# A gated linear unit on one core: the stores of the odd tiles 1 to 29 issued from the sync queue, ahead of the load that waits for the same products

## The chip, the cores and the metric

The kernel runs on one core of a Trainium2 chip. The metric is the device time of one execution in microseconds (us). One execution was profiled as well; the profile's times count from the start of its span.

## The reference

The input x is an array of 8192 x 8192 float32 (268.44 MB). Its left half a is gated by its right half b; the output is 8192 x 4096 float32 (134.22 MB):

```
a, b = np.split(x, 2, axis=-1)
return a * (1 / (1 + np.exp(-b)))
```

Every element is read once and written once, and little is done with it in between.

## The kernel before, in words

**Tiles.** The rows are cut into 32 tiles of 256 rows, two rows to each of the 128 partitions. A tile's load brings 64 KB to each partition (8.39 MB), its store takes 32 KB from each (4.19 MB). In HBM the two rows of a partition lie side by side, so a partition's part of a tile is one contiguous piece. There are two buffers for loads (xs) and two for results (os), used in turn (SLOTS = 2, line 19): tile i uses buffer i % 2.

**What is done with a tile** (function `work`, lines 72 to 100). ScalarE applies the sigmoid to the right half in place (line 92). Then the product is written to the result buffer (line 97) in two pieces: GpSimd takes 1536 of each partition's 8192 results, VectorE the other 6656, one after the other (line 98 makes VectorE's piece follow GpSimd's). On tile 1 VectorE does both pieces. Tiles 0 and 31 are done in four quarters, each with its own activation and product on VectorE, so that work begins and ends on less than a whole tile.

**The waits.** The activation of a middle tile i waits for two things: that load i has landed, and that store i-2 has left the result buffer. They are joined by an empty instruction on TensorE (line 87), which the profile shows as PEldq or PEq. The load of tile i+2 (line 63) goes into the buffer of tile i, so it waits until the products of tile i are done. The store of tile i (line 68) waits for the same products. `place` (line 48) keeps only the waits that are named and keeps each engine's instructions in program order.

**Queues.** Loads are issued from SyncE (nc.sync; the profile's SPq), stores from ScalarE (nc.scalar; ACTq). The profile numbers the DMA queues by who issued: q1 holds SyncE's transfers and q10 ScalarE's. Both are worked off by the same 16 DMA engines.

**Order.** The loop at line 104 goes over the tiles. For each tile it lays down the work, then the load of tile i+2 (line 112), then the stores that are still due (lines 113 and 114). Tile 0's result is stored in two halves, tile 31's in one half and two quarters (lines 37 and 39); all other tiles have one load and one store.

**Start and end.** `_launch_early` (line 117) moves the first load ahead of the kernel's opening barrier. `_close_on_sync` (line 130) rewrites the closing: GpSimd waits for all semaphores but that of the last store from ScalarE's queue, and SyncE waits for that one.

Of the kernel before, what the change touches and what calls it, by code (L numbers as in the profile page):

```python
# [8 lines left out]
def _tiles(ctx, tc, x, out):  # L9
    nc = tc.nc  # L10
    P = nc.NUM_PARTITIONS
    DEP = mybir.DependencyInfo(mybir.DependencyClass.Sync, mybir.DependencyReason.DATA)
    fp32 = mybir.dt.float32
    SIG = mybir.ActivationFunctionType.Sigmoid

    n_rows, n_cols = x.shape
    half = n_cols // 2
    R = 2
    SLOTS = 2
    n_tiles = n_rows // (P * R)  # L20
    x_g = x.rearrange("(g p h r) m -> g h p (r m)", p=P, h=2, r=R)
    out_g = out.rearrange("(g p h r) m -> g h p (r m)", p=P, h=2, r=R)

    pool = ctx.enter_context(tc.tile_pool(name="io", bufs=1))
    xs = [pool.tile([P, R * n_cols], fp32, name=f"x_sb{k}") for k in range(SLOTS)]
    os = [pool.tile([P, R * half], fp32, name=f"o_sb{k}") for k in range(SLOTS)]

    whole = [(0, 8)]
    rows = [(0, 4), (4, 8)]
    cut = half // 16 * 3  # L30
    few_and_most = [(0, 8, 0, cut), (0, 8, cut, half)]
    fourths = [(k, k + 2, k % 4 * half // 4, (k % 4 + 2) * half // 4) for k in range(0, 8, 2)]
    loads = [whole] * n_tiles
    works = [few_and_most] * n_tiles
    stores = [whole] * n_tiles
    behind = [0] * n_tiles
    loads[0] = stores[0] = rows
    works[0] = works[-1] = fourths
    stores[-1] = [(0, 4), (4, 6), (6, 8)]
    behind[-1] = 1  # L40

    def meet(a, b):
        return a[0] < b[1] and b[0] < a[1]

    traced = [[] for _ in range(SLOTS)]
    load_of, mul_of, store_of = {}, {}, {}

    def place(i, ins, *needs):


        kept = {n.ins.name for n in needs}
        for e in traced[i % SLOTS]:
            if e.ins.name not in kept:
                tc.declare_no_dep(ins.ins, e.ins, reason="follows from the waits that are kept")
        traced[i % SLOTS].append(ins)
        tc.keep_in_program_order(ins)
        return ins

    def load(i):
        for lo, hi in loads[i]:  # L60
            c = slice(lo * n_cols // 4, hi * n_cols // 4)
            free = [m for w, m in mul_of.get(i - SLOTS, []) if meet(w, (lo, hi))]
            ins = nc.sync.dma_start(out=xs[i % SLOTS][:, c], in_=x_g[i // 2, i % 2, :, c])  # L63
            load_of.setdefault(i, []).append(((lo, hi), place(i, ins, *free)))

    def store(i, lo, hi):
        c = slice(lo * half // 4, hi * half // 4)
        ins = nc.scalar.dma_start(out=out_g[i // 2, i % 2, :, c], in_=os[i % SLOTS][:, c])  # L68
        done = [m for w, m in mul_of[i] if meet(w, (lo, hi))]
        store_of.setdefault(i, []).append(((lo, hi), place(i, ins, *done)))  # L70

    def work(i, lo, hi, near, far):

        rows = xs[i % SLOTS].rearrange("p (r h m) -> p r h m", r=R, h=2)
        packed = os[i % SLOTS].rearrange("p (r m) -> p r m", r=R)
        r, c = slice(lo // 4, (hi + 3) // 4), slice(near, far)
        b = rows[:, r, 1, c]
        landed = [s for w, s in load_of[i] if meet(w, (lo, hi))]
        gone = [s for w, s in store_of.get(i - SLOTS, []) if meet(w, (lo, hi))]
        middle = 0 < i < n_tiles - 1  # L80
        rest = middle and near
        if rest:
            before = mul_of[i].pop()[1]
        else:
            g = rows[:, r, 1, :] if middle else b
            if middle and gone:
                met = nc.tensor.nop(nofuse=True)  # L87
                for n in (*landed, *gone):
                    tc.add_manual_dep(met.ins, n.ins.name, DEP, reason="joins the waits")
                place(i, met, *landed, *gone)  # L90
                landed = [met]
            before = nc.scalar.activation(out=g, in_=g, func=SIG)  # L92
            for n in landed:
                tc.add_manual_dep(before.ins, n.ins.name, DEP, reason="both have landed")
            place(i, before, *landed)
        engine = nc.gpsimd if far == cut and i > 1 else nc.vector
        mul = engine.tensor_mul(out=packed[:, r, c], in0=rows[:, r, 0, c], in1=b)  # L97
        tc.add_manual_dep(mul.ins, before.ins.name, DEP, reason="follows the gate, or the first columns")
        place(i, mul, before, *(() if middle else gone))
        mul_of.setdefault(i, []).append(((lo, hi), mul))  # L100

    for i in range(SLOTS):
        load(i)
    for i in range(n_tiles):
        due = list(stores[i])
        for k, piece in enumerate(works[i]):
            work(i, *piece)
            ready = works[i][k - behind[i]][1] if k >= behind[i] else 0
            while len(stores[i]) > 1 and k < len(works[i]) - 1 and due[0][1] <= ready:
                store(i, *due.pop(0))  # L110
        if i + SLOTS < n_tiles:
            load(i + SLOTS)
        for lo, hi in due:
            store(i, lo, hi)


def _launch_early(nc):
# [68 lines left out]
@with_exitstack  # L186
def kernel(
    ctx: ExitStack,
    tc: tile.TileContext,
    x: bass.AP,  # L190
    out: bass.AP,
):
    nc = tc.nc
    with ExitStack() as pools:
        _tiles(pools, tc, x, out)
    tc.close()
    tc.compile()
    _launch_early(nc)
    _close_on_sync(nc)
# [30 lines left out]
```

## Time and profile before

| what | value | where |
|---|---|---|
| time, median of 3 runs | 932.57 us (932.52 to 932.69) | the runs |
| the profiled execution's own time | 932.44 us | the runs |
| its span | 931.1 us | the page's head |
| VectorE busy | 232.5 us, 25% | page, part 1 |
| ScalarE busy | 227.0 us, 24% | page, part 1 |
| GpSimd busy | 99.3 us, 11% | page, part 1 |
| bytes moved | 402.67 MB, 432 GB/s over the span | page, parts 2 and 3 |
| activation of a middle tile | 7.03 us | groups by form, line 92 |
| product on GpSimd, on VectorE | 3.42 us, 7.09 us | groups by form, line 97 |
| a load, from issue to landing | 40.0 us, median | page, part 6 |
| a store of a whole tile, from issue to landing | 40.2 us, median | page, part 6 |

The page's first part gives the busy time of the engines that compute: none is busy for more than a quarter of the span. Its second and third parts are about the DMA engines, which all loads and stores share: packets, bytes, and the time for which packets were under way. The chain of waits (part 4) starts at the last instruction and goes back, at each step to what released it. A DMA can be asked about in narrow windows too: how many packets of which queue started in it. A transfer's time "to landing" counts from its issue, so it holds the time in which its packets stood behind others.

### The profile page before, as it was taken

The page shows a single profiled execution, that of the slowest core. Times are in us where ns is not written, and L with a number is a line of the kernel's source. Part 1 is how long each engine was busy: PE and PEld are TensorE (multiplying, and loading weights), DVE is VectorE, ACT ScalarE, POOL GpSimd, SP SyncE. Part 2 cuts the span into 40 slices and gives each one's busy share as a digit, 9 for nine tenths or more (in the row PEclk, how much of TensorE's full clock was granted, in tenths as well). Part 3 has the DMA queues.
Part 4 walks back from the last instruction along what each step waited for, and adds up shares of the span by engine and source line. Part 5 has one row for each costly group of instructions (what it writes and reads, how often), then busy time and mean ns, then how long its engine had stood idle before and what let it go on. Part 6 is the DMA issues. An engine that isn't in the chain of part 4 may idle for free.

```text
span 931.1 us, 299 instructions
## 1 busy us (share of the span) xinstructions
DVE 232.5 (25%) x39; ACT 227.0 (24%) x39; POOL 99.3 (11%) x33
## 2 busy tenths in 40 slices
DVE  1133203332023320233302333023330233311333
ACT  2123332033320333202332023320233202333023
POOL 0001110111101111011110111101111011110110
DMA  9999999999999999999999999999999999999998
GB/s 405 450 442 414 428 450 425 453 405 428 450 428 450 410 469 405 428 450 428 450 405 459 420 428 451 425 450 408 431 448 428 450 408 467 408 428 450 427 452 383
DMA packets 9793, 402.67 MB, mean 432 GB/s; under 512 B 1088, under 2 KB 1088, under 8 KB 1088
## 3 DMA queue, kind: packets, MB, share of 16 engines
q1 hardware_dynamic: 4752, 268.44, 66.6%
q10 hardware_dynamic: 5040, 134.22, 33.4%
q14 instruction: 1, 0.01, 0.0%
HBM read 268.44 MB, written 134.22 MB: 432 GB/s over the span
## 4 chain that ended last, share of the span: by engine, by line
DMA 69%; DVE 12%; ACT 12%; POOL 5%; issue 0%; PEldq 0%; ACTq 0%; SPq 0%
DMA out_dram<-o_sb 60%; DVE o_sb L97 12%; ACT x_sb L92 12%; DMA x_sb<-in_x_dram 9%; POOL o_sb L97 5%; PEldq L87 0%; ACTq L68 0%; SPq L63 0%
## 5 line engine op out<-in xcount | busy, mean ns | idle before, releaser
L97 DVE TENSOR_TENSOR o_sb<-x_sb 128x6656 f32<-128x6656 f32 (+2 forms) x39 | 232.5, 5969 | 690.3 <-POOL o_sb L97 632.7
L92 ACT ACTIVATE x_sb<-x_sb 128x8192 f32<-128x8192 f32 (+1 forms) x38 | 225.7, 5949 | 692.7 <-PEq L87 632.9
L97 POOL TENSOR_TENSOR o_sb<-x_sb 128x1536 f32<-128x1536 f32 x29 | 99.1, 3417 | 793.9 <-ACT x_sb L92 793.9
L92 ACT ACT_TABLE_LOAD x1 | 1.3, 1283 | 0.8 <-PEq L214 0.8
L214 POOL MEMSET const-float32-0.0<- 128x1 f32 x1 | 0.1, 99 | 0.2 <-issue 0.2
L214 POOL MEMSET const-bfloat16-1.0<- 128x1 bf16 x1 | 0.1, 103 | 0.0
L214 POOL MEMSET const-uint8-127<- 128x1 uint8 x1 | 0.1, 103 | 0.0
L214 POOL MEMSET const-float32-1.0<- 128x1 f32 x1 | 0.1, 99 | 0.0
## 6 DMA issues: line engine op xcount, KB each, us to landing
out_dram<-o_sb ACTq DMA_DIRECT2D x30, 4096.0 KB, 40.2
x_sb<-in_x_dram SPq DMA_DIRECT2D x2, 4096.0 KB, 16.6
out_dram<-o_sb ACTq DMA_DIRECT2D x3, 2048.0 KB, 27.8
out_dram<-o_sb ACTq DMA_DIRECT2D x2, 1024.0 KB, 8.3
x_sb<-in_x_dram SPq DMA_DIRECT2D x31, 40.0
```

The costliest lines, as they stand in the source:

```text
L92: before = nc.scalar.activation(out=g, in_=g, func=SIG)
L97: mul = engine.tensor_mul(out=packed[:, r, c], in0=rows[:, r, 0, c], in1=b)
L214: nc = _bacc.Bacc("TRN2", target_bir_lowering=False, num_devices=1)
```

## The change

The stores of tiles 1, 3, 5 to 29 are issued from SyncE instead of ScalarE. For odd tiles the stores that are due are laid down before the load of tile i+2; for even tiles they stay behind it, as before. Tile 31 is odd, but its stores stay on ScalarE's queue; it has no load behind it. The waits that each store and load carry are the same as before.

```
     def store(i, lo, hi):
         c = slice(lo * half // 4, hi * half // 4)
-        ins = nc.scalar.dma_start(out=out_g[i // 2, i % 2, :, c], in_=os[i % SLOTS][:, c])
+        odd = i % 2 and i < n_tiles - 1
+        ins = (nc.sync if odd else nc.scalar).dma_start(out=out_g[i // 2, i % 2, :, c], in_=os[i % SLOTS][:, c])
...
+        if i % 2:
+            for lo, hi in due:
+                store(i, lo, hi)
         if i + SLOTS < n_tiles:
             load(i + SLOTS)
-        for lo, hi in due:
-            store(i, lo, hi)
+        if i % 2 == 0:
+            for lo, hi in due:
+                store(i, lo, hi)
```

## The prediction

> **What bounds the kernel now.** I read the page's DMA queues first, then the stages, then the chain of waits, then the DMA queues in narrow windows. A queue name is that of an issuer: q1 carries what SyncE issues, q10 what ScalarE issues. The columns are packets, MB, and the time the packets took as a share of 16 engines' span.
>
> ```profile
> q1 hardware_dynamic: 4752, 268.44, 66.6%
> q10 hardware_dynamic: 5040, 134.22, 33.4%
> ```
>
> The two shares fill all 16 engines. Each DMA has 16 small completion packets (the page counts 1088 under 512 B for 68 DMAs). q1 keeps 4752 - 33x16 = 4224 data packets of 64 KB (the first two loads: half), q10 5040 - 35x16 = 4480 of 32 KB for whole stores. So each engine gets 8 packets of a load and 8 of a store. 66.6% of 16 x 931.1 us over 4096 packets' worth of 64 KB is 2.42 us each; 33.4% over 4096 worth of 32 KB is 1.215 us. A byte costs the same in either direction and on either queue.
>
> ```profile
> 842.61:871.60 28.99, 7.09 (x1) 7.03 (x1) 3.42 (x1) 1.00 1.00 434
> 871.60:900.61 29.01, 7.09 (x1) 7.03 (x1) 3.42 (x1) 1.00 1.00 434
> ```
>
> In these two stages (one tile each, from the end of one tile's products to the next) the last columns are granted clock, DMA share and GB/s: the DMA engines are at 1.00 and 434 GB/s. 12.58 MB a tile at 434 is 29.0 us, which is the tile's period. So the middle is bound by bytes. What waits there wait only for their turn:
>
> ```profile
> 853.81 0.03 issue
> 853.84 0.06 PEldq L87
> 853.90 0.02 issue
> 853.92 7.04 ACT x_sb L92
> 860.96 0.07 issue
> 861.03 3.43 POOL o_sb L97
> 864.46 0.02 issue
> 864.48 7.10 DVE o_sb L97
> 871.58 0.02 issue
> 871.60 40.04 DMA x_sb<-in_x_dram
> 911.64 0.02 issue
> ```
>
> This is the end of the chain (start, us, what). From a landing to the end of that tile's products is 17.79 us (853.81 to 871.60). The load then issued, tile 31's, needs 40.04 us; at the next tile's products, 900.61, 11.03 us of it are left. Only a DMA engine with nothing to move can lengthen this kernel.
>
> **Who is served first.** Load and store of a tile are issued together and land after 40.0 and 40.2 us: one packet of each in turn. In the window 882.8 to 900.61 both queues start 80 packets. Two rows show how a queue that had been empty joins. The first load is issued at 0.00; no packet starts before 0.97, all 16 engines have started one by 1.6. Tile 0's first store is issued at 18.57, while q1 is busy:
>
> ```profile
> q1 hardware_dynamic: 62, 2.03, 98.1%
> ```
>
> That is the whole of 18.57 to 23.5: loads alone. In 23.5 to 24.0 only q10 starts packets, 16. Available after 0.98 to 1.6 us, as the first load, it was at 19.6 to 20.2; then the packet in service and one more load packet, 64 KB, went first. I read from this that the next packet is already taken when one starts.
>
> **The change, part by part.** 15 stores (tiles 1, 3, ... 29) leave ScalarE's queue, 0.36 us of issue each, and stand on SyncE's queue before the load that needs the same products. What it costs the engines: nothing; SyncE has only issues to do and waits 858.2 us for products, ScalarE is idle 690 us. The load behind the store is issued some 0.36 us later, against 11.03 us of backlog. The store's wait for the products is one that the load behind it has anyway, so nobody is newly held; semaphore instructions beside the issues take 17 ns. On ScalarE the next activation no longer stands behind an odd tile's store; it waits for its own load, which lands later than those products (853.90 against the products' end at 842.61), so that gains nothing.
>
> What moves is the order in the DMA queues. Call an even tile's product end T. Its store starts on an empty q10, soon after T. q1 holds the rest of the odd tile's load, then the load issued at T. An odd tile adds store, then load, both on q1. From about T+33 (8 rounds of 3.63 us after joining) q10 is empty, and q1 alone works through the load, the odd store (8 x 1.215 = 9.7 us) and the next load. Bytes are the same, so two tiles still take 58.0 us as long as q1 doesn't run dry. The even tile's load lands at T+40.2 (its 29.0 us with the store, 11.03 of backlog, a completion), its products end at T+58.0. The odd tile's load lands at about T+14.7 (below), its products end at T+32.5, and at that point 40.2 - 32.5 = 7.7 us are left in the queues against 11.03 now. Less the 0.98 to 1.6 us to a first packet, that still covers. **Middle: 0.** The product ends stand 32.5 and 25.5 us apart instead of 29.0.
>
> One thing in the middle no row shows: a store behind a load in the same queue, with the other queue empty. Below: the engines are at share 1.00 and each byte costs the same both ways, so there is nothing to win. Above: a stop as long as a first packet, 0.98 to 1.6 us, at each of 30 boundaries. Nearest rows: two loads in one queue (4.19 MB each) let their activations start at 12.10 and 21.82, 9.72 us apart, where the bytes at 434 GB/s take 9.67. The last stores follow each other as closely, and in the middle each engine changes direction at every packet. I take 0, and keep 0.1 us each (3 us) for the range.
>
> The Trainium skill, DMA: Bandwidth & Descriptors, section Anatomy of one DMA (SWDGE path), gives each DMA of that path, GpSimd's, some 2 us of fixed cost, mostly a write receipt. If that stopped a queue that is alone, 30 boundaries would give an estimated 60 us. The 9.72 us row speaks against it, for loads.
>
> **The end** is where order counts. Today load 31 lands at 911.64 and store 30, queued behind store 29, has only begun: all its 128 data packets start within 910.6 to 920.3. That work lies beside tile 31's first products:
>
> ```profile
> 911.66 5.51 ACT L92 ACTIVATE x_sb<-x_sb 128x2048 f32<-128x2048 f32 x3 [21.70 <-DMA x_sb<-in_x_dram]
> 913.61 6.70 DVE L97 TENSOR_TENSOR o_sb<-x_sb 128x2048 f32<-128x2048 f32 x3 [13.02 <-ACT x_sb L92]
> 918.13 0.34 ACTq L68 DMA_DIRECT2D out_dram<-o_sb  x1
> ```
>
> Tile 31's first store is issued 6.49 us after the landing, and could start on the last engine at 6.49 + 1.6 = 8.1; store 30 lasts until 9.3 (9.7 us less the 0.35 us from last packets, 911.3, to landing). So the engines never stop, with 1.2 us to spare.
>
> Changed, store 29 is finished by T30 (it went before load 31 on q1) and store 30 meets load 31 alone, packet by packet. Step by step:
> 1. q1 has been alone for 17.79 + 0.35 = 18.1 us at T30 on the last engine: 9.7 for store 29, 8.4 for load 31, that is 3.5 of its 8 packets. 11.03 us remain, as now.
> 2. Store 30 is available 1.6 us later on that engine, in the fifth packet (on the first engine, 0.6 us ahead in its packets, after 0.98 us: also the fifth). The sixth is already taken. So a store packet comes before the seventh, before the eighth, and before load 31's completion packet, which takes a turn (as now: of q1's completions none starts before 910.6, though its last data packets start by 908.5). Three store packets: 3 x 1.215 = 3.6 us.
> 3. Load 31 lands at T30 + 14.7. Of store 30 five packets are left, 6.1 us, so the engines run dry 5.7 us after the landing.
> 4. Tile 31's first store starts at 8.1 after it. The engines stand still for **2.4 us**. Nothing else is left to move. Behind that the last 4.19 MB take their 9.7 us as before; the later pieces, products ready at 8.7 and 11.1 after the landing, are in time.
>
> With n store packets ahead of the completion the stop is 1.215n - 1.3: n=2 gives 1.1, n=3 2.4, n=4 3.6. n=4 needs the store available 0.4 us earlier than I take, n=2 some 2 us later. I choose 3, by the row of tile 0's store. If T30 itself stays where the bytes put it, the sum is 0 + 2.4.
>
> **Sum.** The profiled execution took 932.44 us, 931.1 of it span, 1.34 around it. 932.44 + 2.4 = 934.8; the median of the runs is 0.13 above the profiled execution, so **935.0**.
>
> **Rivals.**
> - *No change that can be measured* (the bound used for the chances is 0.2%, 1.87 us, about what a measurement of this kernel can tell from no change). Mechanism: store 30 is admitted late enough at T30 that load 31 keeps its place, n of 2 or less; the stop is then 1.1 us or nothing, the time 932.6 to 933.7. It decides at 1.215n - 1.3 = 1.87. For: the first store of tile 0 needed 5 us. Against: that wait is explained by two packets, and here two are allowed for. Chance 0.15. The Trainium skill, DMA: Bandwidth & Descriptors, section Issuing engines are not separate DMA queues, speaks for this: it says that choosing another issuer only saves the sequencer's time. By it the time would stay at 932.6. The rows agree for the middle; at the end they show two queues that take turns, and there it leaves out the order.
> - *Stops at the 30 boundaries* on a queue that is alone: 0.98 to 1.6 us each give 29 to 48 us more, 964 to 983. Nothing covers them, since the engines are the bound. For: no row has a store and a load behind each other in one queue. Against: the load rows and the last stores. 0.08, and something small of this kind (0.1 us each, 938.0) lies inside the forecast's upper end.
> - *Faster*: runs of one direction move bytes faster than alternating packets. 0.3% more rate would give 929.8. Against: 2.42 us for 64 KB and 1.215 for 32 KB are the same rate, and loads alone at the start run no faster. 0.05.
> - *The forecast*, n of 3 or 4 and up to 0.1 us a boundary: 0.72.
>
> Slower by over 0.2%: 0.72 + 0.08 = 0.80; within: 0.15; faster: 0.05. The range from 933.1 (n=2, with the shorter first packet of 0.98 us: 932.57 + 0.5) to 938.0 (932.57 + 2.4 + 3) leaves out some 0.1 below and 0.08 above.
>
> **What would show it.** Middle: product ends alternating near 32.5 and 25.5 us, 58.0 a pair, DMA share 1.00 and 434 GB/s in a pair; odd stores landing 17 us after issue, even ones 33. A pair above 58.1 means boundary stops. End: load 31 landing near 14.7 us after T30, a gap of 2 to 4 us without packets before tile 31's first store packet, q10's packets starting some 4 us or more after T30. Wrong would be: T30 later than 901 (the middle lost), an end as dense as now (admission late), or more than 434 GB/s in a pair.

## The result and the profile after

The changed kernel took 940.81 us (median of 4 runs, 940.22 to 946.33), the kernel before 932.63: ratio 1.0101, 95% interval 1.0085 to 1.0117. I had forecast 935.0, with 933.1 to 938.0 as range. The sign was right, the size wrong by more than a factor of three: 8.2 us lost instead of 2.4.

The profiled execution happened to be the longest of the four (946.33); the other three took 940.22 to 940.90. So I read the page from it, and the stages from a second profile of the same kernel (run e4_again below), whose execution took 940.43 us with a span of 939.1. First the DMA queues of the page, as before: packets, MB, share of 16 engines' span.

```profile
q1 hardware_dynamic: 6912, 331.35, 81.9%
q10 hardware_dynamic: 2880, 71.30, 17.5%
```

The bytes have moved over as they should: 63 MB from q10 to q1. But the shares now sum to 99.4% of 945.0 us, 939 us of packets per engine, where before they were 100.0% of 931.1. So the same packets took some 8 us longer, and some 6 us of the span no packet ran. (A share is given to 0.1%, which is 0.9 us.) Two losses, then: **longer packets** and **time without packets**. In the second profile's page the shares are 81.9 and 17.6% of 939.1: 934.4 us of packets (3.3 more than before) and 4.7 us without.

Stages of that second profile: two tiles early, two tiles late, and the end (start:end, length, busy times, clock, DMA share, GB/s).

```profile
121.44:181.73 60.29, 14.18 (x2) 14.06 (x2) 6.83 (x2) 1.00 0.99 428
706.29:764.43 58.14, 14.18 (x2) 14.06 (x2) 6.83 (x2) 1.00 1.00 433
880.96:939.10 58.14, 16.08 (x5) 14.45 (x5) 3.42 (x1) 1.00 0.89 385
```

The share stays near 1.00 in the middle, yet a pair of tiles takes 60.3 us early and 58.1 late, against 58.0 before. A share of 1.00 says that a packet is always under way; it doesn't say how long the packet takes. Nor is the length of a pair the mean loss of the engines: of the load that the early pair waits for, 15 engines write their completion in the window 160 to 162, and the tile's activation starts only at 164.06, when the last engine is done. At the end the share is 0.89. The order of the middle is as forecast: odd stores land 16.2 us after issue (forecast 17), even ones 32.7 (33) in the page's DMA issues.

The end, in the chain of waits of the second profile (start, us, what):

```profile
881.35 39.88 DMA x_sb<-in_x_dram
921.23 0.02 issue
921.25 1.92 ACT x_sb L93
```

Tile 30's products end at 905.07, so load 31 lands 16.2 us later; the forecast had 14.7, before had 11.03. Then the DMA queues in the window 925.75 to 928.5, at its head line:

```profile
DMA packets 0, 0.00 MB, mean 0 GB/s; under 512 B 0, under 2 KB 0, under 8 KB 0
```

For 2.75 us no packet starts on any engine, and the last one before it, which started by 924.55 and takes 1.2 us, is over: tile 31's first store, issued at 927.72, only begins after it. That is the stop of the forecast. But most engines had stopped well before 925.75, because they no longer finish together. Load 31's 16 completion packets, one from each engine, in the kernel before (window 910.6 to 911.4, q1):

```profile
q1 hardware_dynamic: 16, 0.00, 1.1%
```

and in the second profile of the change, in the windows 915 to 918.95 and 915 to 920.95 (all queues; the small ones are the completions, and none of another DMA falls into these windows):

```profile
DMA packets 63, 1.77 MB, mean 448 GB/s; under 512 B 14, under 2 KB 14, under 8 KB 14
DMA packets 88, 2.52 MB, mean 424 GB/s; under 512 B 16, under 2 KB 16, under 8 KB 16
```

Before, all 16 engines end a load within 0.8 us. After, 14 are done by 918.95 and the last two only two us later; the whole spread is near 6 us. The landing is that of the last engine.

### The profile page after: what moved, and what is told of

It is laid out like the page before. It is cut to its first block, busy times and chain, and to the rows that moved or that the text cites. A ratio compares the mean times of both kernels' runs of the same rounds, so it can differ in the third digit from the quotient of the medians.

```text
span 945.0 us, 285 instructions
## 1 busy us (share of the span) xinstructions
DVE 232.5 (25%) x39; ACT 227.0 (24%) x39; POOL 99.3 (11%) x33
## 3 DMA queue, kind: packets, MB, share of 16 engines
q1 hardware_dynamic: 6912, 331.35, 81.9%
## 4 chain that ended last, share of the span: by engine, by line
DMA 69%; DVE 12%; ACT 12%; POOL 5%; SPq 1%; issue 0%; PEldq 0%; ACTq 0%
DMA x_sb<-in_x_dram 69%; DVE o_sb L98 12%; ACT x_sb L93 12%; POOL o_sb L98 5%; SPq L69 1%; PEldq L88 0%; ACTq L69 0%; SPq L63 0%
## 6 DMA issues: line engine op xcount, KB each, us to landing
out_dram<-o_sb SPq DMA_DIRECT2D x15, 4096.0 KB, 16.2
out_dram<-o_sb ACTq DMA_DIRECT2D x15, 4096.0 KB, 32.7
```

## The experiments

All are written on the changed kernel with a function `moved(i)` in place of the test for odd tiles, if not said otherwise: a moved tile's store goes over the sync queue ahead of the load, another's over the scalar queue behind it. Three more kernels leave stores out and move fewer bytes; their times stand in the text.

| run | what goes over the sync queue | us | against before, same chip | ratio, 95% |
|---|---|---|---|---|
| e4_again | the change again | 940.86 | +8.3 | 1.0075 to 1.0126 |
| e1_only29 | store 29 alone | 937.93 | +5.3 | 1.0042 to 1.0072 |
| e2_not29 | odd stores 1 to 27 | 938.12 (to 943.35) | +5.5 | 1.0045 to 1.0098 |
| e3_all_sync | stores 1 to 30 | 938.20 | +5.6 | 1.0044 to 1.0074 |
| f1_only15 | store 15 alone | 934.54 | +1.9 | 1.0013 to 1.0031 |
| f2_last_two | stores 29 and 30 | 935.29 | +2.7 | 1.0017 to 1.0038 |
| f3_behind | odd stores, behind the load | 974.11 | +41.5 | 1.0437 to 1.0472 |
| h1_and_30 | the change and store 30 | 937.92 | +5.3 | 1.0045 to 1.0073 |
| h2_half | odd stores 1 to 13 | 936.98 | +4.4 | 1.0036 to 1.0061 |

### End and middle apart

```
 def moved(i): return i == 29                     # e1_only29
 def moved(i): return i % 2 == 1 and i < 29       # e2_not29
```

> Only the store of tile 29 goes over the sync queue, ahead of load 31; all else as before. This is the end of the change by itself. Theory A (joining: whenever the scalar queue has run empty and gets a store again while loads run on the sync queue, a load packet on every engine takes some 0.5 us longer; and the engines drift apart by it): one such joining, engines still in step, so the stop at the end as I predicted, 2.4 us, plus 0.5: about 935.5. Theory B (the end alone costs what was measured, joining nothing): 938 to 941. Theory C (a load behind a store in one queue stops the engines): 935 plus one boundary or two, under 937.

> The stores of the odd tiles 1 to 27 go over the sync queue, that of tile 29 stays on the scalar queue: the middle of the change by itself, the end as before. Theory A (joining, 14 times 0.5 us): about 7 us slower than before, 938 to 940, and no stop before tile 31's stores. Theory B (the end alone): 932.6. Theory C (28 boundaries in one queue): 5 to 8 us, like A; the next run tells C from A.

One moved store at the end costs 5.3 us; A gave 2.9, C less than 4.4, B 5.4 or more, so none of the three ranges holds it. The middle alone costs 5.5 us (four executions, 937.71 to 943.35), so B (the end is all) falls. The end by itself, in the chain of e1_only29:

```profile
872.25 46.48 DMA x_sb<-in_x_dram
918.73 0.02 issue
```

Load 31 needs 46.48 us where it needed 40.04. From tile 30's products at 900.88 it lands after 17.85 us: 3.2 later than my step 3. The window 923.3 to 926.0 holds no packet at all: the stop is there. A little wider, the window 922.05 to 926.05 holds nothing but the 16 completions of store 30, the last of them before 923.3:

```profile
q10 hardware_dynamic: 16, 0.00, 0.2%
```

In 926.0 to 926.3 all 16 engines start tile 31's first store. So each engine stands still for some 3 to 4 us, more than the 2.4 of the forecast. Load 31's completions show why: eight come in 916.0 to 916.5 and eight in 917.3 to 918.45, 1.2 us apart, as long as one store packet. I read from this that on half of the engines four store packets went ahead of the completion and not three; the prediction's own formula gives 3.6 us for n=4.

### Is it store 30 between load 31's packets?

```
 def moved(i): return i in (29, 30)                              # f2_last_two
 def moved(i): return i % 2 == 1 and i < n_tiles - 1 or i == 30  # h1_and_30
```

> The stores of tiles 29 and 30 go over the sync queue, so that store 30 stands behind load 31 in one queue and can't go between its packets; all else as before. If the end cost of the run with tile 29 alone (5.3 us) comes from store 30's packets that go ahead of load 31 (my step 2): load 31 lands 11 to 13 us after tile 30's products instead of 17.9, the engines don't stop before tile 31's stores, and 1 to 2.5 us of longer packets are left: 933.6 to 935. If it came from longer packets at the change of direction in one queue: about as slow as tile 29 alone, 937 to 938.

```profile
872.28 42.23 DMA x_sb<-in_x_dram
914.51 0.02 issue
```

With store 30 behind load 31 in the same queue, the load lands at 914.51, 4.2 us sooner than in e1_only29, and q1 works on through 914.2 to 921.8 with a share of 96.8%. The time falls by 937.93 - 935.29 = **2.6 us**. That is what the order at the end costs, net. It is not the stop itself, which was longer, because this kernel has a long packet of its own: load 31's last packets, ahead of store 30 in q1 (window 908.8 to 910.1), have 273.9% of 1.3 us, 3.56 each instead of 2.42. What is left, 2.7 us, is longer packets, with no stop that matters. All three figures lie a little above what I expected (landing 13.6 us after the products against 11 to 13, 2.7 against 1 to 2.5, 935.29 against 933.6 to 935).

> The change, and the store of tile 30 over the sync queue as well, where it stands behind load 31. If the change's loss is the sum of two parts, store 30 going between load 31's packets (2.6 us, the run with tile 29 alone less that with 29 and 30) and longer packets with drift in the middle (5.5 us, the run without tile 29): 940.8 less 2.6, 938.2. If the drift makes the stop at the end whatever the order: 940 to 941.

937.92: taking store 30 out of load 31's way gives 2.9 us back from the change too. So the loss is about a sum: 5.5 in the middle and 2.6 at the end make 8.1, measured 8.2. The fit to 0.1 is luck, since the executions of the change, of e2_not29 and of h1_and_30 range over 2 us and more.

### What lengthens packets in the middle?

```
 def moved(i): return 0 < i < n_tiles - 1         # e3_all_sync
```

> The stores of all tiles 1 to 30 go over the sync queue, each ahead of the load that waits for the same products; only tile 0's and tile 31's stay on the scalar queue. The scalar queue is empty from about 70 us to the end, so nothing joins a busy queue until the last stores, and there are 60 boundaries between a load and a store in one queue instead of 30. Theory A (joining): no lengthened packets in the middle, two tiles in 58.0 us, 932.6 to 934. Theory C (boundaries): twice the middle cost of the change, 945 or more.

Neither came. Nothing joins from the other queue here, and yet 5.6 us are lost; with twice the boundaries, but not twice the loss. The page's shares, 97.6 and 2.1% of 936.9 us, are 934.1 us of packets on the mean engine, 3.0 more than before; the rest is time without packets. At the first store that follows a load in q1, the window 96.3 to 97.0 holds one load packet from each engine, the last of its load:

```profile
q1 hardware_dynamic: 16, 1.05, 405.7%
```

405.7% of 0.7 us is 2.84 us a packet, against 2.42. Late in the run such packets are back at 2.42, while the engines' completions of one load, within 0.4 us at first, spread over 5.6 us from the middle of the run on. The end waits for the last of them.

Two kernels were meant to price each kind of meeting by itself: one in which q10 runs empty and joins loads again 15 times, and one in which only q1 is used.

```
 for i in range(n_tiles):
     due = list(stores[i])
+    if i % 2 and i < n_tiles - 1: due = []       # f4_no_odd, on the kernel before
+    if i % 2 == 0 and i > 0: due = []            # g2_no_even, on the change
```

> The stores of the odd tiles 1 to 29 are left out altogether (63 MB of the output are not written), the rest as before: the scalar queue runs empty between even stores and joins again 15 times, and no queue ever holds a load and a store. The bytes left, 339.7 MB, take 787.5 us by before's rate with its own start and end. If joining by itself lengthens packets (theory A): two tiles take 48.3 us plus 0.3 to 0.7, and load packets longer than 2.42 us show where even stores begin. If only the change of direction in one queue does it: 48.3 us a pair and no longer packets.

> The change, with the stores of the even tiles 2 to 30 left out (63 MB of the output are not written): the scalar queue is empty, so nothing joins, and 15 odd stores stand between loads in one queue, with engines that stop now and then and so stay in step. It gives the price of the change of direction in one queue by itself. By the run with all stores on the sync queue: 0.4 us of longer packets on the mean engine per store, beside 1.3 where a store joins from the other queue. If it is as dear as joining: 1.3 here too. If the all-sync run owed its longer packets to drift alone: under 0.1.

f4_no_odd took 823.06 and 827.35 us in its two executions, well above the 787.5 of its bytes. Two tiles there take 50.5 us instead of 48.3 (stage 241.68 to 292.19, DMA share 0.98). Load packets just ahead of a joining store, window 293.1 to 294.4 (16 of them, and one small packet):

```profile
q1 hardware_dynamic: 17, 1.05, 284.1%
```

284.1% of 1.3 us is 3.69 us instead of 2.42, 1.3 us more on the mean engine, here and at nearly all the other places. The rest of the 2.2 us is time in which engines have nothing to move. But this is not the price of joining a busy queue, which the run was meant to give. Load and store are both issued at 292.19, and in 291.1 to 293.1 only completions start: the engines have run dry, and the long packet is the first after that. A first packet from rest is long with no store about. The first packets of the kernel before (window 0.95 to 1.6, 16 of 32 KB) have 287.8% of 0.65 us, 1.87 us instead of 1.215. So f4_no_odd prices **a start from rest with a store beside it, 1.3 us**, and leaves open what part of that is the store's. g2_no_even (822.15 us, one execution) has no joining. Its last packet of a store ahead of a load, and the first of that load (with 16 completions), in the windows 327.9 to 328.55 and 329.65 to 330.85:

```profile
q1 hardware_dynamic: 16, 0.52, 302.4%
```

```profile
q1 hardware_dynamic: 32, 1.05, 219.8%
```

302.4% of 0.65 us is 1.97 us for 32 KB instead of 1.215; 219.8% of 1.2 is 2.64 for 64 KB instead of 2.42. Together **1.0 us for going from a store to a load in one queue**, at this place. I had expected 0.4.

Neither price holds in the change itself. In its second profile I take the first store that was moved and the first one that joins, where all 16 engines are still in step. These are the last store packets ahead of a load in q1 (window 78.28 to 78.68), and the load packets under way when the store joins (window 91.6 to 92.0):

```profile
q1 hardware_dynamic: 16, 0.52, 303.4%
q1 hardware_dynamic: 16, 1.05, 688.9%
```

303.4% of 0.4 us is 1.21 us: going from a store to a load costs nothing here. 688.9% of 0.4 us is 2.76 us: joining costs 0.34. At the next load packets ahead of a moved store (window 125.6 to 126.4, 302.2%) it is 2.42 again, so nothing there either. Both kinds of meeting can lengthen packets, then, but by amounts that differ from run to run; in the change it is the joining that shows.

Does joining need a store?

```
 for i in range(n_tiles):
     due = list(stores[i])
+    if 0 < i < n_tiles - 1: due = []
...
-            ins = nc.sync.dma_start(out=xs[...
+            ins = (nc.scalar if i % 2 else nc.sync).dma_start(out=xs[...
```

> The stores of tiles 1 to 30 are left out (all of the output but the first and last tile is not written), and the odd tiles' loads go over the scalar queue: loads alone, but a queue that has run empty joins a busy one at every tile. It tells joining from direction. If joining a busy queue lengthens packets whatever it carries: load packets longer than 2.42 us by 0.5 to 1 us where the other queue begins, as in the run without odd stores (1.3 us of longer packets on the mean engine at each joining). If only a store among loads does: all load packets 2.42 us. The time itself, some 640 to 680 us, tells neither.

It took 691.27 us, above the 640 to 680 expected, and doesn't answer the question. With so few bytes one queue ends as the other begins: q1's completions stand in 277.2 to 278.25, and q10's load, issued at 277.37, starts in the window 278.3 to 279.25 on engines that have just run dry (15 of its packets here, and one small one of q1):

```profile
q10 hardware_dynamic: 15, 0.98, 307.7%
```

307.7% of 0.95 us, for 16 engines with 15 packets, is 3.12 us a packet, 0.7 longer than 2.42. That is a start from rest again, and as much longer as the first packets of the kernel before (1.87 instead of 1.215). Whether a load that joins running loads makes them longer stays open.

### Why 15 moves don't cost 15 times one move

```
 def moved(i): return i == 15                     # f1_only15
 def moved(i): return i % 2 == 1 and i < 14       # h2_half
```

> Only the store of tile 15, in the middle, goes over the sync queue ahead of its load; beginning and end as before. Theory A+C (a queue that is alone and goes from loads to a store, and a store that joins while loads run, make load packets longer, by different amounts on the 16 engines; the engines never stand still in the middle, so what an engine has lost it never makes good): the slowest engine loses 1 to 2.5 us there, its lag stays to the end, 933.8 to 935. Theory B (the end alone): 932.6.

1.9 us, as theory A+C had it. The place where store 16 joins, window 495.45 to 496.15, 16 load packets:

```profile
q1 hardware_dynamic: 16, 1.05, 478.1%
```

3.35 us instead of 2.42, and no engine has run dry here: in this run joining costs 0.9 us. Store 15's last packets (1.57 us instead of 1.215, window 484.2 to 484.8) and the next packets of some engines add to it. And it stays: from there on everything is late, and nothing makes up for it.

> Only the stores of tiles 1 to 13 go over the sync queue, 7 of the 15; from tile 14 on all is as before. If each move costs alike (5.5 us by 14): 2.8 us, 935.4. If the first moves are dear and later ones cheap, because engines that have drifted apart no longer meet at the same moment (1.9 us for one move alone): 936 to 938. In both cases the engines stay apart to the end, since nothing lets the last one catch up.

936.98, +4.4: seven moves cost four fifths of what fourteen cost. After tile 14 each pair takes 58.0 us again, and the engines keep the 3.8 us by which they have come apart (load 31's 16 completions fill the window 913.4 to 917.4). So the first moves are dear, the later ones cheap.

What goes with it is how far the engines are in step. In the second profile of the change, with engines over 3 to 6 us, late pairs cost 0 to 0.5, and the load packets at its last joining (window 906.1 to 908.3, 109.9%) take 2.42 us. In the first profile of the change, the long execution, 12 of the 16 engines complete load 31 within 0.7 us (window 920 to 920.7) and the rest up to 6 us later:

```profile
DMA packets 25, 0.46 MB, mean 655 GB/s; under 512 B 12, under 2 KB 12, under 8 KB 12
```

and there pairs cost as much late as early:

```profile
182.73:241.43 58.70, 14.18 (x2) 14.06 (x2) 6.83 (x2) 1.00 1.00 429
710.40:769.20 58.80, 14.18 (x2) 14.06 (x2) 6.83 (x2) 1.00 1.00 427
```

There the load packets at a late joining (window 559.7 to 560.85, 16 of them, 266.5%) take 3.06 us. That would also explain why one execution of the same kernel took 5.5 us longer than three others. I have not set the engines' spread on purpose, so this is what goes together, not a cause shown. It isn't all, either: at the first joining of the second profile the engines were in step, and it cost 0.34 us, against 0.9 in f1_only15.

### The queue without the order

```
-        if i % 2:
+        if False:                                # stores always behind the load
```

> The odd stores go over the sync queue as in the change, but behind the load, not ahead of it: the queue moved without the order. The scalar queue still runs empty between even stores, so packets still get longer where stores join or follow loads, and engines drift; at the end load 31 is not behind store 29, is done earlier, and store 30 hardly meets it. Theory A+C: 935 to 938, no stop at the end for store 30's sake. If the order ahead of the load is what costs: within 1 us of before.

I was wrong: 974.11 us, 41.5 lost where theory A+C allowed at most 5.4. The odd store now stands behind a load of 19.3 us, and the tile two later waits for it, since it needs the result buffer. Two windows over the middle, whose lengths I chose; read their last columns, DMA share and GB/s:

```profile
636.00:694.00 58.00, 14.19 (x2) 14.06 (x2) 6.83 (x2) 1.00 1.00 423
694.00:756.00 62.00, 14.19 (x2) 14.06 (x2) 6.83 (x2) 1.00 0.97 408
```

Odd stores are issued at 669.85, 731.85 and 790.83, so pairs take 62.0 and 59.0 us in turn instead of 58.0. The odd products end at 731.5 and the load ahead lands just after (its activation starts at 733.10), so when the next two DMAs are issued hardly anything is left in the queues. The engines run dry (share 0.97). The first load packets after that (window 732.3 to 733.2, 350.3%) take 3.15 us instead of 2.42, and the last ones ahead of an odd store (window 688.0 to 690.2, 166.1%) 3.65. So of the two parts of the change, the order ahead of the load is the part that keeps the queue move bearable.

### The second look

> The changed kernel once more, nothing altered, for a second profile: the profiled execution took 946.33 us and three others 940.2 to 940.9. Theory A with drift as an accident of one execution: 940 to 941, completions of a load's 16 engines within 2 us of each other, a shorter stop at the end. If the drift belongs to the kernel, this profile too shows engines 4 to 7 us apart.

940.86, range 939.86 to 945.04: the change again, with the spread in this profile too, so it belongs to the kernel. How large it is differs from execution to execution.

## Why the prediction was wrong

- **What bounds the kernel** (bytes at 434 GB/s, so only an engine with nothing to move can lengthen it): right about the bound, wrong in its last sentence. Packets can be under way and last longer. I took 2.42 and 1.215 us, means of a steady alternation, as properties of the bytes.
- **Middle: 0** is the step that failed. I named the unknown, bounded it from above by 0.98 to 1.6 us at each of 30 boundaries and took 0, because two loads and several stores follow each other without loss and because each engine alternates at every packet. None of these rows has a change after a run of one kind. Measured: 5.5 us by 14 moves, 0.4 a move, where the range kept 0.1 for each of a move's two boundaries. No stop shows there (share 0.99 to 1.00). Packets get longer, in the change's own profile where the other queue joins (2.76 us instead of 2.42 at first), and the end waits for the engine that has lost most. The kernel before had a hint: tile 0's first store also joins running loads, and the load packets ahead of it (window 20.79 to 21.39, 16 of them with 16 completions) have 427.2% of 0.6 us, 2.56 each instead of 2.42. I used that very place for the time of admission and did not look at the packets' length.
- **Stops at the 30 boundaries** as a rival (29 to 48 us) looked at the wrong place. With all stores in one queue such a boundary does lengthen packets (2.84 us instead of 2.42 at first), but in the change's second profile the boundaries that I read cost nothing (1.21 and 2.42 us). The joining from the other queue, which costs something there, was in no rival.
- **The end, 2.4 us:** the mechanism was right: store 30 goes between load 31's packets, and the engines then run dry. f2_last_two against e1_only29 (2.6) and h1_and_30 against the change (2.9) show what that order costs. That these come so close to 2.4 is in part luck. The stop itself, in e1_only29, is 3 to 4 us, as for n=4; the net is smaller because the other order has long packets of its own. Step 3 was off: load 31's landing, forecast 14.7 us after the products, came at 17.85 with store 29 alone moved and at 13.56 with store 30 out of the way too. The time until an idle engine starts tile 31's first store, taken as 0.98 to 1.6, was 0.8 to 1.0 (issue 927.72, no packet up to 928.5, 15 engines begun by 928.7).
- **One term was missing altogether:** I let all engines run alike, 0.6 us apart. A landing waits for the last of 16, and engines that didn't stop didn't make good what they had lost: in h2_half they are still 3.8 us apart at the end, 18 tiles after the last move.
- **The shape of the middle** was right: the bytes, the alternating order, the landings after 17 and 33 us. It had no bearing on the time.

The Trainium skill, DMA: Bandwidth & Descriptors, section Issuing engines are not separate DMA queues, says that the choice of issuer only saves the sequencer's time. By that rule the time would have stayed; the same bytes from other queues took 8.2 us more here, and 41.5 more in another order. Its section Latency and other measured facts gives some 0.6 us from a DMA by SyncE or ScalarE to its first byte; the runs here show 0.8 to 1.0 from issue to the first packet on idle engines, of which the issuing instruction itself takes 0.34 (927.72 to 928.06).

What stays open: what inside a DMA engine lengthens a packet when the stream changes, why by nothing at one place and by 0.9 us at another, and whether being out of step is what makes later changes cheaper. No run here shows any of these.

## What to carry to other kernels

In a kernel that is bound by DMA, two queues that are never empty and take turns packet by packet were the best found here; a queue that runs dry and joins again, or one that carries loads and stores in turn, costs from nothing to about 1 us per meeting while the DMA share stays at 1.00, and only the time of a packet (share times window over packets) shows it. At the end, put the last store that isn't needed behind the last load that is: store 30 between load 31's packets cost 2.6 us.

## What the runs showed of the hardware that was not expected

- The packet under way can become longer when another stream begins: 3.35 us instead of 2.42 when a store joins loads from the other queue (f1_only15; 2.76 at first in the change), 2.84 to 3.56 for the last load packet ahead of a store in its own queue (e3_all_sync, f2_last_two), 1.97 instead of 1.215 for a store's last packet ahead of a load (g2_no_even). Where I read the change's second profile, the last two cost nothing.
- An engine's first packet after it has run dry is long: 1.87 us instead of 1.215 at the start of the kernel before, 3.12 instead of 2.42 in g1_loads_two_queues.
- The 16 engines, within 0.4 to 0.6 us of each other throughout the kernel before, come apart by 3 to 6 us in the change and stay so to the end.
